# GpSimd's work in the token mixers in order of emission, stores issued by the engine that wrote them, and mixer transfers asked for some turns later

## Chip, cores and metric

The kernel runs on one core of one Trainium2 chip. The metric is the time of one execution on the device in microseconds; the number to beat is the median of three runs. Engines are named as in the profile: PE (matrix products), DVE (VectorE), ACT (ScalarE), POOL (GpSimd) and SP (SyncE, which here does nothing but issue transfers; SPq is its queue).

## What is computed

One layer of a hybrid encoder on a prompt of 512 frames and a sample of 64 frames, model width 2048, all in float32. The reference, cut to what matters here:

```python
def gdn_step(s, blk):            # 8 heads, 128 x 128 state
    q, k, v, g, beta = blk
    ...
    lower = jnp.where(strict, jnp.einsum('bhid,bhjd->bhij', kb, k) * decay, 0.0)
    rhs = jnp.concatenate([v * beta, kb * jnp.exp(big_g)[..., None]], axis=-1)
    sol = lax.linalg.triangular_solve(eye + lower, rhs, left_side=True, lower=True, unit_diagonal=True)
    ...

def token_mixers(h, ...):
    proj = h @ w_in
    ...
    o_a = from_heads(o_a, gla_norm) * jax.nn.silu(a_r)          # gated linear attention, 4 heads
    qkv, conv_new = causal_dwconv(concat([b_q, b_k, b_v]), st_conv, gdn_conv_w)
    q = l2norm(to_heads(c_q, GDN_HEADS)) * GDN_DK ** -0.5
    k = l2norm(to_heads(c_k, GDN_HEADS))
    ...
    o_b = from_heads(o_b, gdn_norm) * jax.nn.silu(b_g)          # gated DeltaNet, 8 heads
    return concat([o_a, o_b]) @ w_out, ...

def trunk(x, c, ...):
    mod = silu(c) @ w_ada + b_ada
    x = x + g1 * token_mixers(rmsnorm(x, norm1) * (1 + sc1) + sh1, ...)
    x = x + g2 * conv_ffn(rmsnorm(x, norm2) * (1 + sc2) + sh2, ...)
    return rmsnorm(x, final_norm), ...
```

## The kernel before

All activations are kept transposed, 128 features on the partitions by 2 x 288 frames (256 of the prompt and 32 of the sample in each half). A weight tile is loaded by SP, split by ACT into a high part and by DVE into a rest (lines 599 and 600), and each 128 x 128 tile takes six matmuls (`mm6`, lines 512 and 514): the "product matmuls" below.

The program has a head (modulation, normalization), then the mixer stage, then the output projection, and the FFN, in which nothing changes. In the mixer stage `in_tile` computes one projection tile of 128 columns after the other, 16 tiles of weights each, and calls `tick` after each of these 16. A tick gives one turn to the list of jobs (`job_step`) and now and then one step to the w_ada sums (`ada_block`: load 512 KB into one of two buffers `xr`, line 764, then four sums on DVE, line 772). A job is a generator, one for each head (`gdn` for the eight DeltaNet heads and for the sample, `gla` for the four attention heads). The list is walked from the oldest job; a job that yields WAIT lets the next one have the turn as well, a plain `yield` ends the turn. `rest(n)` yields WAIT n times: so many turns in which others run, while data gets ready.

For each DeltaNet head h the tiles come in the order q(h+1), k(h+1), v(h), gate(h), and q, k and v pass through `gdn_conv`: ACT and DVE copy the tile to `cb`, POOL sets its edges (lines 916 and 917) and saves its last columns (918, 919), then ACT (920), three sums on DVE (922), silu on ACT (924). A job of `gdn` then does this: a row of sums of log decays is loaded and made into decay matrices (ACT, POOL's selects 178 and 179); k and q are transposed (line 144), squared, and raised to -1/2 by POOL (`rsqrt`, lines 137 and 138); after a rest the block matrix `a` is made (216), and `inverse16` inverts its 32 diagonal 16 x 16 blocks: `a` is stored to DRAM (340), loaded as 32 lanes (345), worked on by POOL in 14 steps of two instructions (351, 352), copied (354), stored again (355) and loaded as columns `cm` (358), from which DVE builds two matrices (362). PE then joins the blocks to a whole inverse (238, 244, 253, 258), takes v (its transposes, 144), runs through four blocks of frames (276 to 305), and the outputs are squared, raised by POOL (138) to normalize them, transposed (144), multiplied by the gate and stored (`put_o`, 929), to be loaded again by `load_o` (1077) in the output projection. The sample's 64 columns of each tile go to DRAM by `put_s` (900), and are taken up by the jobs of the sample.

The order in which each engine issues its instructions is fixed when the program is built. A list scheduler takes instructions by priority (the order of emission, with weight splits and the jobs' DVE and ACT work moved ahead by 80) as soon as its own estimate says that they can run. Each engine then works strictly in that order, and so does each engine that issues transfers: an instruction that waits holds up everything behind it. All transfers stand in SP's queue.

Of the kernel before, what the change touches and what calls it, by code (L numbers as in the profile page):

```python
# [12 lines left out]
ALU = mybir.AluOpType  # L13
# [18 lines left out]
JOB_RATE, ADA_RATE = 1.0, 0.65  # L32


REST_D, REST_X, REST_T, REST_N, REST_G = 8, 16, 3, 2, 3
LATE = 3
N_EARLY = 4
N_EXTRA = 24
# [57 lines left out]
class Kern:  # L96
    def __init__(self, tc, ctx, i, o):
        self.tc, self.nc, self.ctx, self.i, self.o = tc, tc.nc, ctx, i, o
        self.n = 0
        self.cp = ctx.enter_context(tc.tile_pool(name="cp", bufs=1, side="left"))  # L100
        self.pg = ctx.enter_context(tc.tile_pool(name="pg", bufs=2, space=PSUM))
        self.c = {}
        self.jv, self.ja = _Sooner(tc, tc.nc.vector), _Sooner(tc, tc.nc.scalar)

    def load_consts(self, pool, names):
        nc = self.nc
# [28 lines left out]
    def rsqrt(self, out, src, n, parts=P):  # L135

        self.nc.vector.tensor_scalar_add(out[:parts, :n], src[:parts, :n], EPS)
        self.nc.gpsimd.tensor_tensor(out[:parts, :n], out[:parts, :n], self.mhalf[:parts, :n], op=ALU.pow)  # L138

    def transpose4(self, src4, n=4):  # L140

# [13 lines left out]
    def gdn(self, qF, kF, x, gain, hcols, gb_src, s0, s_out, o_put, last_level):  # L155
# [19 lines left out]
            A.activation(du[:, b], gb[:, b], AF.Relu, bias=gcol[:, b:b + 1], scale=-1.0)  # L175
        A.activation(dl, dl, AF.Exp, scale=-1.0)
        A.activation(du, du, AF.Exp, scale=-1.0)
        nc.gpsimd.affine_select(du, du, pattern=[[0, 4], [1, P]], compare_op=ALU.is_ge, fill=0.0, base=0, channel_multiplier=-1)
        nc.gpsimd.affine_select(dl, dl, pattern=[[0, 4], [-1, P]], compare_op=ALU.is_gt, fill=0.0, base=0, channel_multiplier=1)
        if pair:  # L180
            nc.gpsimd.memset(du[0:64, :, 64:P], 0.0)
        A.activation(gb, gb, AF.Exp)
        for b in range(4):
            A.activation(dl[:, b], dl[:, b], AF.Copy, scale=nbeta[:, b:b + 1])
# [136 lines left out]
        while "gate" not in x:  # L321
            yield WAIT
        V.tensor_tensor(kn, kn, x["gate"](), op=ALU.mult)
        o_put(kn)

    def rest(self, n):
# [4 lines left out]
    def inverse16(self, a):  # L331

        nc, c, G = self.nc, self.c, self.nc.gpsimd
        pitch = 4 * P
        d0 = self.dp.tile([8 * (16 * pitch + 16)], F32, tag="d0", bufs=2, name=self.name("d0"))
        d1 = self.dp.tile([2, 32, 256], F32, tag="d1", bufs=2, name=self.name("d1"))
        nc.sync.dma_start(d0[:P * pitch].rearrange("(p f) -> p f", p=P), a.rearrange("p b t -> p (b t)"))  # L340
        lane = self.m()[:32].rearrange("p (w f) -> p w f", w=2)
        xx, xt = [lane[:, n].rearrange("p (i j) -> p i j", i=16) for n in range(2)]
        blocks = d0.rearrange("(n f) -> n f", n=8)[:, :16 * pitch].rearrange("n (i b j) -> n i b j", i=16, b=4)
        for b in range(4):
            nc.sync.dma_start(xx[8 * b:8 * b + 8], blocks[:, :, b, :16])
        yield from self.rest(REST_D)
        G.memset(lane[:, 0, 0:256:17], 1.0)
        for i in range(1, 15):
            rest = slice(i + 1, 16)
            sh = [32, 15 - i, i]  # L350
            G.tensor_tensor(xt[:, rest, :i], xx[:, rest, i:i + 1].to_broadcast(sh), xx[:, i:i + 1, :i].to_broadcast(sh), op=ALU.mult)  # L351
            G.tensor_tensor(xx[:, rest, :i], xx[:, rest, :i], xt[:, rest, :i], op=ALU.add)  # L352
            yield WAIT
        G.tensor_copy(xt, xx.rearrange("p i j -> p j i"))
        nc.sync.dma_start(d1.rearrange("w q f -> q w f"), lane)
        cm = self.sp.tile([P, 2, 4, 16], F32, tag="cm", bufs=1, name=self.name("cm"))
        for w in range(2):
            nc.sync.dma_start(cm[:, w], d1[w].rearrange("(b n) (i j) -> (n i) b j", b=4, i=16))
        sh = [P, 4, 8, 16]
        t, u = self.m4(), self.m4()  # L360
        for w, x in enumerate((t, u)):
            nc.vector.tensor_tensor(x.rearrange("p b (n j) -> p b n j", n=8), cm[:, w].unsqueeze(2).to_broadcast(sh),
                                    c["bd16"].rearrange("p (n j) -> p n j", n=8).unsqueeze(1).to_broadcast(sh), op=ALU.mult)
        yield from self.rest(REST_X)
        return u, t

    def gla(self, nb, qF, kF, g, x, s0, s_out, o_put):
# [103 lines left out]
        for f in range(2):  # L471
            dst = (qd, kd3)[f]
            while f"gate{f}" not in x:
                yield WAIT
            V.tensor_tensor(dst, dst, x[f"gate{f}"](), op=ALU.mult)
            o_put(f, dst)


    def tick(self):
# [416 lines left out]
    def put_s(self, name, col, write):  # L896

        t = self.sp.tile([P, TS], F32, tag="ts", bufs=4, name=self.name("ts"))
        write(t)
        self.nc.sync.dma_start(self.sd[name][:, col * TS:(col + 1) * TS], t)  # L900

    def get_s(self, name, w=512):

# [4 lines left out]
    def gdn_conv(self, ps, t, dst, name, h):  # L908
# [4 lines left out]
        acc = self.ap.tile([P, 582], F32, tag="ca", bufs=1, name=self.name("ca"))  # L913
        A.activation(cb[:, 3:515].rearrange("p (h t) -> p h t", h=2), ps[:, :, :HP], AF.Copy)
        V.tensor_copy(cb[:, 518:582].rearrange("p (h t) -> p h t", h=2), ps[:, :, HP:HT])
        nc.gpsimd.tensor_copy(cb[:, 0:3], self.zero3)
        nc.gpsimd.tensor_copy(cb[:, 515:518], self.vmap["st_conv"].rearrange("p (i t) -> p t i", i=3)[:, t])
        nc.gpsimd.tensor_copy(self.cs[:, 0, :, t], cb[:, 512:515])
        nc.gpsimd.tensor_copy(self.cs[:, 1, :, t], cb[:, 579:582])
        A.activation(acc[:, :579], cb[:, 0:579], AF.Copy, scale=self.vec("gdn_conv_w", t))  # L920
        for j in range(1, 4):
            V.scalar_tensor_tensor(acc[:, :579], cb[:, j:j + 579], self.vec("gdn_conv_w", 24 * j + t), acc[:, :579],
# [701 lines left out]
        return g  # L1624


class _States:


# [55 lines left out]
```

## Time and profile before

| | before |
|---|---|
| three runs, us | 2977.28, 2977.57, 2982.16; median 2977.57 |
| the profiled execution, us | 2988.47, of which the span of the profile is 2986.8 |
| mean granted clock of PE | 0.978 |
| transfers | 395.55 MB, mean 132 GB/s |
| PE's busy tenths in 40 slices | 6998899999899999999999999999999999999998 |
| POOL's busy tenths | 0004342232210000000011011111101100000000 |

A row of the timeline gives start and length in us, engine, line, operation and tiles, then in brackets how long the engine was idle before it and what ended that. A row of the waits gives engine and line, what it waited for, the total in us, how often, and the longest. Line 1623 is the helper through which all DVE and ACT work of the jobs goes, so such work is told by its tiles.

### The profile page before, as it was taken

What the parts mean: (1) busy time and instruction counts of PE and PEld (TensorE: products, weight loads), DVE (VectorE), ACT (ScalarE), POOL (GpSimd) and SP (SyncE); (2) the same over time, 40 slices, a digit from 0 to 9 for tenths busy, and PEclk for the clock granted to TensorE, in tenths of its full rate; (3) what the DMA queues carried; (4) which work ended last, traced back from release to release, by engine and by line L of the source; (5) the groups of instructions that cost most, each with busy time, mean ns of one, the idle gap of its engine ahead of it and who ended that gap; (6) DMA issues with size and microseconds to landing.
All of it is one profiled execution on the core that took longest, in us unless ns stands there. A gap on an engine that the chain in (4) does not pass through costs nothing.

```text
span 2986.8 us, 52415 instructions
## 1 busy us (share of the span) xinstructions
PE 2871.2 (96%) x21096; PEld 2774.8 (93%) x21096; DVE 2048.5 (69%) x3198; ACT 1198.7 (40%) x2062; POOL 334.5 (11%) x609
## 2 busy tenths in 40 slices
PE   6998899999899999999999999999999999999998
PEld 3688889999799998999999999999999999999997
DVE  2355776667568867557888888888888865555555
ACT  4235454444435433245444444444444421222223
POOL 0004342232210000000011011111101100000000
PEclk7999999999899999999999999999999999999999
DMA  8964554445454446743333333333333473333221
GB/s 251 286 191 118 143 161 130 129 129 147 123 156 131 140 128 184 201 141 97 111 104 105 113 100 106 113 104 104 114 106 104 133 235 101 111 101 115 86 80 65
DMA packets 535446, 395.55 MB, mean 132 GB/s; under 512 B 59657, under 2 KB 465412, under 8 KB 535204
## 3 DMA queue, kind: packets, MB, share of 16 engines
q1 hardware_dynamic: 535204, 392.21, 44.7%
q8 instruction: 166, 2.72, 0.4%
q14 instruction: 76, 0.62, 0.1%
HBM read 356.47 MB, written 35.67 MB: 131 GB/s over the span
## 4 chain that ended last, share of the span: by engine, by line
PE 80%; DVE 6%; DMA 4%; POOL 4%; ACT 3%; issue 2%; SPq 0%; ACTq 0%; POOLq 0%; DVEq 0%
PE g L512 25%; PE g L514 13%; PE bank L1301 11%; PE bank L1300 11%; PE bank L1302 11%; DVE acc L772 2%; DMA xr<-in_w_ada_dram 1%; PE bank L144 1%; PE bank L672 1%; POOL m L352 1%; POOL m L351 1%; POOL s L138 1%; PE bank L405 1%; PE bank L778 1%; ACT m L1623 1%
## 5 line engine op out<-in xcount | busy, mean ns | idle before, releaser
L1301 PE MATMUL bank<-slot,wh 128*128 128x290 f32 x2464 | 736.2, 299 | 0.0
L1300 PE MATMUL bank<-slot,wh 128*128 128x290 f32 x2464 | 733.9, 298 | 0.0
L1302 PE MATMUL bank<-slot,wl 128*128 128x290 f32 x2464 | 728.0, 295 | 0.0
L512 PE MATMUL g<-slot,wh 128*128 128x288 f32 x3168 | 551.6, 295 | 0.2 <-DVE slot L1070 0.2
L512 PE MATMUL g<-hh,wh 128*128 128x288 f32 x2048 | 470.0, 308 | 2.4 <-ACT wh L599 2.4
L1302 PEld LDWEIGHTS bank<-slot,wl 128*128 128x128 f32 x2464 | 470.6, 191 | 0.0
L1301 PEld LDWEIGHTS bank<-slot,wh 128*128 128x128 f32 x2464 | 469.7, 191 | 0.1
L512 PEld LDWEIGHTS g<-slot,wh 128*128 128x128 f32 x3168 | 465.8, 188 | 0.7 <-DVE slot L1070 0.5
L1300 PEld LDWEIGHTS bank<-slot,wh 128*128 128x128 f32 x2464 | 464.1, 188 | 0.1
L514 PE MATMUL g<-hh,wl 128*128 128x288 f32 x2048 | 461.9, 304 | 1.2 <-DVE wl L600 1.2
L599 ACT ACTIVATE wh<-raw 128x1024 fp32r<-128x1024 f32 x215 | 227.2, 1058 | 586.6 <-PE g L512 571.4
L512 PE MATMUL g<-hl,wh 128*128 128x288 f32 x2048 | 460.6, 304 | 0.0
L1070 DVE SCALAR_TENSOR_TENSOR slot<-g,mod,slot 128x512 f32<-128x512 f32 (+1 forms) x448 | 201.9, 491 | 287.9 <-PE g L514 286.3
L772 DVE SCALAR_TENSOR_TENSOR acc<-xr,ct,acc 128x512 f32<-128x512 f32 x480 | 341.5, 754 | 29.0 <-DMA xr<-in_w_ada_dram 28.1
L512 PEld LDWEIGHTS g<-hh,wh 128*128 128x128 f32 x2048 | 337.7, 193 | 14.7 <-issue 10.2
L514 PEld LDWEIGHTS g<-hh,wl 128*128 128x128 f32 x2048 | 338.9, 193 | 8.3 <-issue 6.0
L514 PE MATMUL g<-slot,wl 128*128 128x288 f32 x1584 | 342.8, 295 | 0.0
L512 PEld LDWEIGHTS g<-hl,wh 128*128 128x128 f32 x2048 | 338.9, 193 | 4.1 <-issue 3.7
L600 DVE TENSOR_TENSOR wl<-raw,wh 128x1024 fp32r<-128x1024 f32 x215 | 262.0, 1219 | 64.9 <-ACT wh L599 63.3
L1247 ACT ACTIVATE wh<-raw 128x1024 fp32r<-128x1024 f32 x176 | 186.0, 1057 | 222.6 <-PE bank L1301 194.2
L514 PEld LDWEIGHTS g<-slot,wl 128*128 128x128 f32 x1584 | 255.3, 188 | 0.0
L1248 DVE TENSOR_TENSOR wl<-raw,wh 128x1024 fp32r<-128x1024 f32 x176 | 215.4, 1224 | 54.0 <-ACT wh L1247 54.0
(346 smaller groups left out, 3180.4 us busy)
## 6 DMA issues: line engine op xcount, KB each, us to landing
raw<-in_w_up_dram SPq DMA_DIRECT2D x176, 512.0 KB
xr<-in_w_ada_dram SPq DMA_DIRECT2D x128, 512.0 KB
raw<-in_w_in_dram SPq DMA_DIRECT2D x100, 512.0 KB
raw<-in_w_down_dram SPq DMA_DIRECT2D x88, 512.0 KB
hraw<-in_w_ada_dram SPq DMA_DIRECT2D x64, 512.0 KB
raw<-in_w_out_dram SPq DMA_DIRECT2D x32, 512.0 KB
slot<-actd SPq DMA_DIRECT2D x44, 288.0 KB
actd<-v SPq DMA_DIRECT2D x44, 256.0 KB
```

Source lines behind the costliest of these rows:

```text
L138: self.nc.gpsimd.tensor_tensor(out[:parts, :n], out[:parts, :n], self.mhalf[:parts, :n], op=ALU.pow)
L512: T.matmul(ps[:, h if bank is None else bank, :n], wh, x[:, h, :n], start=f, stop=False)
L514: T.matmul(ps[:, h if bank is None else bank, :n], wl, ah[:, h, :n], start=False, stop=stop)
L599: nc.scalar.activation(hi[:, :n_], raw[:, :n_], AF.Copy)
L600: nc.vector.tensor_tensor(lo[:, :n_], raw[:, :n_], hi[:, :n_].bitcast(F32), op=ALU.subtract)
L772: V.scalar_tensor_tensor(acc[s], w[:, k], col, acc[s], op0=ALU.mult, op1=ALU.add)
L1070: self.nc.vector.scalar_tensor_tensor(x1[:, :, z], ps[:, :, c], gain[:, q:q + 1], x1[:, :, z], op0=ALU.mult, op1=ALU.add)
L1247: self.nc.scalar.activation(hi, src, AF.Copy)
L1248: self.nc.vector.tensor_tensor(lo, src, hi.bitcast(F32), op=ALU.subtract)
L1300: T.matmul(ps, wh[:, j], hi, start=(c < 3 and j == 0), stop=False, skip_group_check=True)
L1301: T.matmul(ps, wh[:, j], lo, start=False, stop=False, skip_group_check=True)
L1302: T.matmul(ps, wl[:, j], hi, start=False, stop=(j == NPAIR - 1), skip_group_check=True)
```

## The change

POOL's work in the mixers goes through a helper, `_InTurn`, which ties each POOL instruction to the one emitted before it, so that the scheduler keeps them in the order of emission. The stores of `put_s` are issued by ACT, which wrote the tile (the log decays `ag`, which DVE writes, stay on SP), and the store of the inverted blocks by POOL. The rests around the transfers of `inverse16` are distributed anew: 2 turns before `a` is stored, 3 before it is loaded, 7 before POOL begins, 3 before the result is loaded, 5 before DVE uses it and 6 before PE does; before, these were 0, 0, 8, 0, 0 and 16. Five turns of rest stand before a head's output is stored. No computing instruction is added; 60 transfers change their engine.

```diff
-REST_D, REST_X, REST_T, REST_N, REST_G = 8, 16, 3, 2, 3
+REST_S, REST_L, REST_D, REST_X, REST_U, REST_T, REST_N, REST_O, REST_G = 2, 3, 7, 5, 6, 3, 2, 5, 3
...
         self.jv, self.ja = _Sooner(tc, tc.nc.vector), _Sooner(tc, tc.nc.scalar)
+        self.pool = _InTurn(tc, tc.nc.gpsimd)
...
-        self.nc.gpsimd.tensor_tensor(out[:parts, :n], out[:parts, :n], self.mhalf[:parts, :n], op=ALU.pow)
+        self.pool.tensor_tensor(out[:parts, :n], out[:parts, :n], self.mhalf[:parts, :n], op=ALU.pow)
...
         V.tensor_tensor(kn, kn, x["gate"](), op=ALU.mult)
+        yield from self.rest(REST_O)
         o_put(kn)
...
-        nc, c, G = self.nc, self.c, self.nc.gpsimd
+        nc, c, G = self.nc, self.c, self.pool
...
+        yield from self.rest(REST_S)
         nc.sync.dma_start(d0[:P * pitch].rearrange("(p f) -> p f", p=P), a.rearrange("p b t -> p (b t)"))
+        yield from self.rest(REST_L)
...
-        nc.sync.dma_start(d1.rearrange("w q f -> q w f"), lane)
+        G.dma_start(d1.rearrange("w q f -> q w f"), lane)
+        yield from self.rest(REST_L)
...
+        yield from self.rest(REST_X)
         t, u = self.m4(), self.m4()
...
-        yield from self.rest(REST_X)
+        yield from self.rest(REST_U)
         return u, t
...
-        self.nc.sync.dma_start(self.sd[name][:, col * TS:(col + 1) * TS], t)
+        (self.nc.sync if name == "ag" else self.nc.scalar).dma_start(self.sd[name][:, col * TS:(col + 1) * TS], t)
...
-        nc.gpsimd.tensor_copy(cb[:, 0:3], self.zero3)
+        self.pool.tensor_copy(cb[:, 0:3], self.zero3)
...
+class _InTurn:
+    def __init__(self, tc, engine):
+        self.tc, self.engine, self.last = tc, engine, None
+    def __getattr__(self, name):
+        f = getattr(self.engine, name)
+        def g(*a, **kw):
+            with self.tc.issue_after(self.last) if self.last is not None else nullcontext():
+                r = f(*a, **kw)
+            self.last = self.tc.nc.cur_bb.bb.instructions[-1]
+            return r
+        return g
```

The other calls of `nc.gpsimd` in `gdn` (selects and one memset) and in `gdn_conv` (the copies of lines 917 to 919) are replaced in the same way, and in `gla` the two output stores come together after the rest.

The first place where the order moves is POOL around the output norm of the second DeltaNet head. Before, its power (`s_546`) stands behind the end of the third head's inverse (`m_3489`):

```order
L352 TENSOR_TENSOR m_3489<-m_3489 32x3x12
L351 TENSOR_TENSOR m_3489<-m_3489 32x2x13
L352 TENSOR_TENSOR m_3489<-m_3489 32x2x13
L351 TENSOR_TENSOR m_3489<-m_3489 32x14
L352 TENSOR_TENSOR m_3489<-m_3489 32x14
L354 COPY m_3489<-m_3489 32x256
L138 TENSOR_TENSOR s_546_3687<-s_546_3687,mhalf 128x4
```

In the changed kernel the same power is called `s_545` and the third head's inverse `m_3741` (line 1648 is the helper, for all of POOL's mixer work):

```order
L1648 TENSOR_TENSOR rq_3297<-rq_3297,mhalf 128x4
L1648 COPY cb_3490<-zero_100 128x3
L1648 COPY cb_3490<-cols 128x3
L1648 COPY cs<-cb_3490 128x3 x2
L1648 TENSOR_TENSOR s_545_3681<-s_545_3681,mhalf 128x4
L1648 MEMSET m_3741 32x16
L1648 TENSOR_TENSOR m_3741<-m_3741 32x14 x2
```

The power has moved from behind the 28 steps and the copy of the inverse to ahead of its first instruction; it is so for all heads.

The second place is SP's queue after the lanes of the second head's inverse are asked for. Before, the store of the inverted blocks (`d_368`) and the load of the columns (`cm`) stand here, with loads of w_ada (`xr`) and w_in (`raw`) between them:

```order
L345 DMA m_2542<-d_367_2539 8x16x16 x4
L764 DMA xr_2743<-in_w_ada_dram 128x2x512
L764 DMA xr_2823<-in_w_ada_dram 128x2x512
L598 DMA raw_3389<-in_w_in_dram 128x8x128
L355 DMA d_368_2540<-m_2542 32x2x256
L764 DMA xr_2919<-in_w_ada_dram 128x2x512
L358 DMA cm_3107<-d_368_2540 128x4x16 x2
L764 DMA xr_2978<-in_w_ada_dram 128x2x512
```

Now, from just behind the load of the lanes on (lines are nine higher here and the load of `cm` is line 364):

```order
L773 DMA xr_2727<-in_w_ada_dram 128x2x512
L773 DMA xr_2811<-in_w_ada_dram 128x2x512
L773 DMA xr_2897<-in_w_ada_dram 128x2x512
L773 DMA xr_2971<-in_w_ada_dram 128x2x512
L773 DMA xr_3030<-in_w_ada_dram 128x2x512
L607 DMA raw_3377<-in_w_in_dram 128x8x128
L311 DMA out_dram<-st_2908 128x128
L773 DMA xr_3108<-in_w_ada_dram 128x2x512
L939 DMA od_71<-m_2092 256x1x256
L607 DMA raw_3507<-in_w_in_dram 128x8x128
L773 DMA xr_3287<-in_w_ada_dram 128x2x512
L364 DMA cm_3162<-d_366_2536 128x4x16 x2
```

The store has left the queue, and seven w_ada loads instead of three stand between the lanes and the columns.

The third place is POOL where the sixth head's k and q are normalized (`s_709`, `rq_4946`) and v of the fifth passes the convolution. Before (`cb_5147` is v's buffer):

```order
L919 COPY cs<-cb_4870 128x3
L916 COPY cb_5147<-zero_100 128x3
L917 COPY cb_5147<-cols 128x3
L138 TENSOR_TENSOR s_709_4921<-s_709_4921,mhalf 128x4
L138 TENSOR_TENSOR rq_4946<-rq_4946,mhalf 128x4
L918 COPY cs<-cb_5147 128x3
```

And now (`cb_5141` is v's buffer):

```order
L1648 AFFINE_SELECT m_4901<-m_4901 128x512
L1648 TENSOR_TENSOR s_709_4921<-s_709_4921,mhalf 128x4
L1648 TENSOR_TENSOR rq_4946<-rq_4946,mhalf 128x4
L1648 COPY cb_5141<-zero_100 128x3
L1648 COPY cb_5141<-cols 128x3
L1648 COPY cs<-cb_5141 128x3 x2
```

The two copies that set the edges of v's buffer have moved behind the powers of k and q. In PE's order the transposes of the sixth and seventh head's q and k stand 41 and 50 product matmuls later than before, and those of the fifth head's v 47 product matmuls behind the first of these, where it was 79.

More of the change, by code (lines that the diff above doesn't have):

```diff
@@ L177, in gdn @@
         A.activation(du, du, AF.Exp, scale=-1.0)
-        nc.gpsimd.affine_select(du, du, pattern=[[0, 4], [1, P]], compare_op=ALU.is_ge, fill=0.0, base=0, channel_multiplier=-1)
-        nc.gpsimd.affine_select(dl, dl, pattern=[[0, 4], [-1, P]], compare_op=ALU.is_gt, fill=0.0, base=0, channel_multiplier=1)
+        self.pool.affine_select(du, du, pattern=[[0, 4], [1, P]], compare_op=ALU.is_ge, fill=0.0, base=0, channel_multiplier=-1)
+        self.pool.affine_select(dl, dl, pattern=[[0, 4], [-1, P]], compare_op=ALU.is_gt, fill=0.0, base=0, channel_multiplier=1)
         if pair:
-            nc.gpsimd.memset(du[0:64, :, 64:P], 0.0)
+            self.pool.memset(du[0:64, :, 64:P], 0.0)
         A.activation(gb, gb, AF.Exp)
@@ L475, in gla @@
             V.tensor_tensor(dst, dst, x[f"gate{f}"](), op=ALU.mult)
-            o_put(f, dst)
+        yield from self.rest(REST_O)
+        for f in range(2):
+            o_put(f, (qd, kd3)[f])
     def tick(self):
@@ L915, in gdn_conv @@
         V.tensor_copy(cb[:, 518:582].rearrange("p (h t) -> p h t", h=2), ps[:, :, HP:HT])
[L916 to L919, printed above, removed]
+        self.pool.tensor_copy(cb[:, 0:3], self.zero3)
+        self.pool.tensor_copy(cb[:, 515:518], self.vmap["st_conv"].rearrange("p (i t) -> p t i", i=3)[:, t])
+        self.pool.tensor_copy(self.cs[:, 0, :, t], cb[:, 512:515])
+        self.pool.tensor_copy(self.cs[:, 1, :, t], cb[:, 579:582])
         A.activation(acc[:, :579], cb[:, 0:579], AF.Copy, scale=self.vec("gdn_conv_w", t))
```

## Prediction

> **What bounds the kernel now.** I read the shares of the page first, then busy time by stretch, then the matrix engine's (PE's) own gaps, then the rows of other engines around the largest gaps, and last the queue of SP.
>
> ```profile
> PE 2871.2 (96%) x21096; PEld 2774.8 (93%) x21096; DVE 2048.5 (69%) x3198; ACT 1198.7 (40%) x2062; POOL 334.5 (11%) x609
> 200.00:1300.00 1100.00, 1034.90 (x7585) 992.37 (x7584) 748.75 (x1307) 490.46 (x1113) 211.12 (x433) 0.97 0.52 146
> 1600.00:2000.00 400.00, 400.00 (x2976) 400.00 (x2975) 333.39 (x408) 179.84 (x214) 44.25 (x54) 1.00 0.37 106
> ```
>
> PE is the bound: 96% of the span. In the FFN (1600 to 2000 us; columns: length, then busy time and count of PE, weight loads, DVE, ACT, POOL, then granted clock, DMA share, GB/s) it has no gap, one matmul in 400/2976 = 0.134 us. The change touches the mixer stage alone, roughly 200 to 1300 us, where PE is idle for 1100 - 1034.9 = 65 us at a granted clock of 0.97. So the change can only work on those 65 us and on the clock there. These are the largest gaps (in brackets, idle time ahead and what ended it):
>
> ```profile
> 240.13 0.48 PE L144 MATMUL bank<-consts,m 128*128 128x128 f32 x1 [3.53 <-ACT m L1623]
> 280.57 0.48 PE L144 MATMUL bank<-consts,m 128*128 128x128 f32 x1 [5.46 <-ACT m L1623]
> 314.80 0.80 PE L276 MATMUL bank<-st,m 128*128 128x128 f32 x2 [6.13 <-DVE st L1623]
> 389.22 0.47 PE L144 MATMUL bank<-consts,m 128*128 128x128 f32 x1 [6.42 <-ACT m L1623]
> 454.88 0.44 PE L144 MATMUL bank<-consts,m 128*128 128x128 f32 x1 [2.57 <-ACT m L1623]
> 566.44 1.09 PE L144 MATMUL bank<-consts,qkv 128*128 128x128 f32 x8 [2.36 <-ACT qkv L924]
> 640.91 1.09 PE L144 MATMUL bank<-consts,qkv 128*128 128x128 f32 x8 [1.51 <-ACT qkv L924]
> 766.33 0.47 PE L144 MATMUL bank<-consts,m 128*128 128x128 f32 x1 [10.31 <-ACT m L1623]
> ```
>
> After a gap PE also runs slowly for some microseconds (the granted clock is the third number from the end):
>
> ```profile
> 314.80:319.40 4.60, 4.60 (x23) 4.55 (x24) 3.50 (x6) 1.67 (x8) 0.00 (x0) 0.61 0.36 92
> 389.20:393.80 4.60, 4.58 (x21) 4.57 (x22) 1.47 (x3) 1.53 (x4) 0.00 (x0) 0.53 1.05 263
> 454.90:458.50 3.60, 3.60 (x16) 3.58 (x17) 1.37 (x2) 3.02 (x7) 0.00 (x0) 0.53 0.27 38
> 766.30:772.30 6.00, 5.97 (x26) 5.96 (x27) 4.19 (x7) 1.54 (x4) 0.00 (x0) 0.50 0.50 153
> 566.40:574.40 8.00, 7.96 (x40) 7.96 (x41) 4.19 (x9) 4.11 (x21) 3.46 (x4) 0.57 0.68 195
> 642.00:650.00 8.00, 8.00 (x43) 7.98 (x42) 1.34 (x5) 3.89 (x19) 1.01 (x1) 0.57 0.25 67
> ```
>
> **Part 1: POOL in order of emission, and the inverse's store off SP's queue.** Two gaps show POOL's order directly. At 389 us:
>
> ```profile
> 381.62 0.27 DVE L137 TENSOR_SCALAR s<-s 128x4 f32<-128x4 f32 x1
> 387.15 0.59 POOL L354 COPY m<-m 32x256 f32<-32x256 f32 x1
> 387.72 1.01 POOL L138 TENSOR_TENSOR s<-s,mhalf 128x4 f32<-128x4 f32 x1
> ```
>
> The small power (line 138) that ends a head's output norm has its input at 381.9 and starts at 387.7, right behind the last instruction of the next head's 16x16 inverse. Four ACT copies and the transposes of PE wait for it. Now that power stands ahead of the whole inverse (first place shown in the order), so what is left is the chain itself, as where nothing blocked it:
>
> ```profile
> 835.31 0.33 PE L144 MATMUL bank<-consts,m 128*128 128x128 f32 x1 [0.78 <-ACT m L1623]
> ```
>
> So 389 gives 6.42 - 0.8 = 5.6 us. At 454 the pair stands alike in the chain of work:
>
> ```profile
> 452.81 0.59 POOL m L354
> 453.40 0.99 POOL s L138
> ```
>
> 2.57 - 0.8 = 1.8 us. Two gaps come by way of SP:
>
> ```profile
> 743.73 0.37 SPq L598 DMA_DIRECT2D raw<-in_w_in_dram  x1
> 758.26 0.33 SPq L355 DMA_DIRECT2D d<-m  x1
> 758.68 0.38 SPq L764 DMA_DIRECT2D xr<-in_w_ada_dram  x1
> 762.82 1.41 DVE L772 SCALAR_TENSOR_TENSOR acc<-xr,ct,acc 128x512 f32<-128x512 f32 x2 [9.01 <-DMA xr<-in_w_ada_dram]
> 313.07 1.41 DVE L772 SCALAR_TENSOR_TENSOR acc<-xr,ct,acc 128x512 f32<-128x512 f32 x2 [6.46 <-DMA xr<-in_w_ada_dram]
> ```
>
> SP issues nothing for 14 us, until the inverse is finished and its store (L355) can go; the load of w_ada stands behind that store, DVE stands still 9.0 us for the load, and behind DVE's wait stands the norm that PE waits for. The same at 313 us (6.5 us). The store is now issued by POOL, behind its own copy, and SP has seven w_ada loads ahead of the load that needs it (second place). I take both gaps as gone but for the chain: 10.31 - 0.8 = 9.5 and 6.1 us. Idle time won: 5.6 + 1.8 + 9.5 + 6.1 = **23.0 us**. The slow clock behind these four, length times what is missing to 1: 4.6 x 0.39 + 4.6 x 0.47 + 3.6 x 0.47 + 6.0 x 0.50 = 1.8 + 2.2 + 1.7 + 3.0 = **8.7 us**.
>
> **Part 2: stores of the sample columns from ACT.** 51 stores move from SP to ACT, and the nine of the inverse to POOL.
>
> ```profile
> SPq L355 <- POOL m L354: 74.5, 8, 14.0
> SPq L900 <- ACT ts L925: 35.0, 16, 4.0
> SPq L358 <- DMA d<-m: 10.7, 8, 3.0
> ```
>
> (SP's waits: total, times, longest.) SP loses the first two waits. ACT pays at most 51 x 0.33 (the issue at 758.26) = 17 us, in a stage in which it is busy 490 of 1100 us; I cost it at nothing, hidden beside PE, and at 17 us if every store stood ahead of something PE waits for. A store from POOL is not in the trace. Nearest rows: landing of the same store from SP, 10.7/8 = 1.3 us to 3.0 us. I take 3 us. Its cover: the inverse's result is ready here (two products on DVE) long before PE first uses it,
>
> ```profile
> 393.03 1.29 DVE L362 TENSOR_TENSOR m<-cm,consts 128x512 f32<-128x512 f32 x2 [0.28 <-DMA cm<-d]
> 421.96 1.00 PE L238 MATMUL bank<-m,m 128*128 128x64 f32 x8
> ```
>
> 27.6 us, so nothing; without cover, 9 x 3.0 = 27 us. The Trainium skill (SBUF — State Buffer, "SBUF: two separate sides") says of a DMA issued by GpSimd that its descriptors cannot be written while VectorE runs a two-port operation, and that such a DMA belongs on ACT or SP. It gives 3.1 us for one held so; nine would be 28 us, an estimate from that page, on the same cover. No row here shows such a store.
>
> **Part 3: the rests.** From the block matrix to the first use of the inverse the rests come to 2+3+7+3+5+6 = 26 turns, before 8+16 = 24, and five are added ahead of the output store. A turn is six product matmuls, 0.8 us. Two turns before the use delay only when PE does that work, not how much it does. The five at the end lie here:
>
> ```profile
> 1173.72 2.52 SPq L934 DMA_DIRECT2D od<-m  x4
> 1261.28 5.29 SPq L1077 DMA_DIRECT2D raw<-od  x2
> ```
>
> The last store of head outputs goes 87 us before the next loads of them, against 4 us of rest: nothing. But PE's order shifts: the transposes of a new head's q and k (gaps at 566 and 641) stand 41 and 50 product matmuls later, 5.5 and 6.7 us, more than they waited. They could give 2.36 + 1.51 plus the clock of two windows, 2 x 8.0 x 0.43 = 6.9, in all 10.8 us. I take half, **5.4 us**, since their input (the convolution of k) now stands behind the exponentials on ACT, whose load may be late in SP's queue. The gaps of heads 0 and 1 at 240 and 281 us (9.0 us) hang on DVE, ACT and POOL together, and the power of q still stands behind the first inverse; I take a third, **3 us**.
>
> **What it adds.** POOL's strict order puts the first two copies of v's convolution (L916, L917) behind the powers of the next head's k and q (third place). Before:
>
> ```profile
> 565.88 1.02 POOL L916 COPY cb<-zero 128x3 f32<-128x3 f32 x1 [5.49 <-DVE ca L922]
> 573.54 1.01 POOL L138 TENSOR_TENSOR rq<-rq,mhalf 128x4 f32<-128x4 f32 x1 [2.52 <-DVE rq L137]
> 584.19 0.77 ACT L920 ACTIVATE ca<-cb,cols 128x579 f32<-128x579 f32 x1
> 589.62 0.63 ACT L924 ACTIVATE qkv<-ca 128x512 f32<-128x512 f32 x1 [4.66 <-DVE ca L922]
> 590.30 0.66 PE L144 MATMUL bank<-consts,qkv 128*128 128x128 f32 x4
> ```
>
> The power of q ends 574.55 - 566.44 = 8.1 us after the transposes of q and k begin. Two copies, 0.4 to 2.0 us; then from L920 to the end of L924 6.1 us: v is ready 14.6 to 16.2 us after them. PE comes to v's transposes after 47 product matmuls (79 before), 6.3 us, and the head's own matmuls. Those took 23.9 - 79 x 0.134 - 3.4 of slow clock = 9.9 us before. So PE arrives at 16.2 us, with 0 to 1.6 us to spare. With DVE's other work in between I expect about 1 us of waiting for seven heads, and 2 us of slow clock behind two of them: 7 + 4 = **11 us** lost; bounds 0 and 40 (4 us and half the heads' clock).
>
> **Sum.** 23.0 + 8.7 + 5.4 + 3 - 11 = 29 us of the profiled span of 2986.8. That execution took 2988.47, 0.37% over the median of 2977.57; scaled by that, 29 stays 29: **2948 us**.
>
> **Rivals.**
> - *All of it goes well*: parts 1 and 3 in full and no wait for v: 23.0 + 8.7 + 10.8 + 9.0 = 51.5 us, 2926. For it: SP's queue is nearly free of waits. Against: a tight chain for v in each head.
> - *SP's wait only moves*: the load of the inverse's result (L358) still stands in SP's queue and waits for POOL's chain and the slower store, with weights and w_ada behind it. If that brings back the gaps at 314 and 766, 6.1 + 9.5 + 1.8 + 3.0 = 20.4 us return: gain 9, 2969. Against: it is asked for three turns after the store.
> - *Only issue time is saved*: 60 issues of 0.33 us on engines beside PE, nothing on the path, and new gaps for old: 2977. The Trainium skill (DMA: Bandwidth & Descriptors, "Issuing engines are not separate DMA queues") says that spreading DMAs over engines saves just the time to issue them. The 74.5 us above speak against it: here the queue's order is what waits.
> - *v late, slower*: POOL holds v's copies longer than PE leaves room. At 4 us for seven heads and 3.4 us of slow clock behind each, 52 us instead of 11: 12 us slower, 2989. It decides from 2.4 us for each head on (7 x 5.8 us is the whole gain).
>
> **How the numbers follow.** About 0.2% (6 us) can be told from no change. Forecast (gain of 15 to 42 us) 0.52; all goes well 0.16; SP's wait moves 0.16; only issue time 0.06; v late 0.10. Faster 0.84, same 0.06, slower 0.10. The range reaches from 2926, the first rival, to 2974, past the second; it leaves out the last two and little below.
>
> **What would show it.** Right: no gap over 2 us ahead of a head's last transposes (L144 behind the power); no DVE wait for w_ada behind the inverse; SP's waits for POOL a fraction of 74.5 us; PE idle in the stage near 40 us instead of 65, clock 0.98 or more. Wrong: gaps ahead of the transposes of v released by L924, POOL's copies L916 starting late behind L138, or SP standing long at L358.

## Result and the profile after

The change made the kernel **slower by 0.6%**: 2997.61 us (median of four runs, 2996.68 to 2998.48) beside 2979.86 us of the kernel before on the same chip, ratio 1.0062 with a 95% interval of [1.0046, 1.0078]. The prediction was 2948 us with a range to 2974 and 0.84 for faster; it was wrong in sign. The profiled execution took 2998.38 us with a span of 2996.7, which is 9.9 us more than the profiled execution of before. The medians lie 17.8 us apart, since the profiled execution of before lay 8.6 us above this median and that of the changed kernel 0.8 us above its own.

In the changed kernel lines stand some higher: the transposes (144) are 146, the row load (170) is 172, the inverse's store, lanes and columns `cm` (340, 345, 358) are 344, 350 and 364, DVE's products of `cm` (362) are 369, w_ada's load and sums (764, 772) are 773 and 781, and the convolution (914, 915, 920, 922, 924) is 924, 925, 930, 932 and 934. Line 1633 is the jobs' DVE and ACT work, and 1648 all of POOL's mixer work.

First the busy time by stretch of the changed kernel (columns as in the prediction: length, busy time and count of PE, weight loads, DVE, ACT, POOL, granted clock, DMA share, GB/s), for the stage and for 8 us behind two gaps:

```profile
200.00:1300.00 1100.00, 1025.78 (x7488) 983.63 (x7487) 744.44 (x1296) 480.32 (x1105) 221.54 (x442) 0.96 0.50 144
578.50:586.50 8.00, 8.00 (x36) 8.00 (x37) 4.11 (x8) 3.23 (x13) 0.92 (x1) 0.50 0.65 184
742.80:750.80 8.00, 7.99 (x51) 7.99 (x51) 2.28 (x5) 3.99 (x16) 1.03 (x1) 0.72 0.47 131
```

PE is idle 74.2 us in the stage (1100 - 1025.78) instead of 65.1, and the clock is a hundredth lower instead of higher. What PE and the others wait for (changed kernel; total, times, longest):

```profile
PE bank L146 <- ACT qkv L934: 35.3, 7, 8.5
PE bank L146 <- ACT m L1633: 11.3, 12, 3.8
SPq L364 <- DMA d<-m: 68.2, 9, 10.2
ACT m L1633 <- DMA m<-gd: 33.7, 7, 9.6
DVE m L369 <- DMA cm<-d: 43.6, 10, 7.9
DVE acc L781 <- DMA xr<-in_w_ada_dram: 16.2, 21, 1.9
```

The same waits in the kernel before:

```profile
PE bank L144 <- ACT m L1623: 33.4, 13, 10.3
PE bank L144 <- ACT qkv L924: 5.4, 3, 2.4
ACT m L1623 <- DMA m<-gd: 10.3, 5, 3.2
DVE m L362 <- DMA cm<-d: 15.3, 5, 6.1
DVE acc L772 <- DMA xr<-in_w_ada_dram: 28.1, 17, 9.0
```

The last transposes' wait for the normalized output fell by 22.1 us, as meant. This is what became of the gaps at 389, 454 and 766 us (PE of the changed kernel):

```profile
380.78 0.33 PE L146 MATMUL bank<-consts,m 128*128 128x128 f32 x1 [1.19 <-ACT m L1633]
454.39 0.33 PE L146 MATMUL bank<-consts,m 128*128 128x128 f32 x1 [0.79 <-ACT m L1633]
776.54 0.33 PE L146 MATMUL bank<-consts,m 128*128 128x128 f32 x1 [0.69 <-ACT m L1633]
```

The wait of the next head's k and q transposes for the convolution of k (L934) rose by 29.9 us. How that came, in the head around 510 to 580 us, from the timelines of PE, POOL, SP, DVE and ACT of the changed kernel (start, length, engine; idle time ahead in brackets):

```profile
578.48 1.97 PE L146 MATMUL bank<-consts,qkv 128*128 128x128 f32 x8 [7.19 <-ACT qkv L934]
...
532.23 1.01 POOL L1648 TENSOR_TENSOR s<-s,mhalf 128x4 f32<-128x4 f32 x1 [19.90 <-DVE s L139]
533.25 5.93 POOL L1648 TENSOR_TENSOR m<-m 32x14 f32<-32x14 f32 x16
547.39 1.45 POOL L1648 COPY cs<-cb 128x3 f32<-128x3 f32 x2 [7.20 <-ACT cb L924]
548.79 8.03 POOL L1648 TENSOR_TENSOR m<-m 32x54 f32<-32x54 f32 x12
557.79 0.62 POOL L1648 DMA_DIRECT2D d<-m  x1 [0.29 <-POOL m L1648]
...
520.66 1.40 SPq L350 DMA_DIRECT2D m<-d  x4
548.86 0.37 SPq L607 DMA_DIRECT2D raw<-in_w_in_dram  x1
559.79 0.37 SPq L364 DMA_DIRECT2D cm<-d  x1
561.87 0.53 SPq L172 DMA_DIRECT2D m<-gd  x1
...
561.72 1.30 DVE L369 TENSOR_TENSOR m<-cm,consts 128x512 f32<-128x512 f32 x2 [5.56 <-DMA cm<-d]
567.74 0.22 DVE L925 COPY cb<-g 128x64 f32<-128x64 f32 x1
...
568.00 0.99 ACT L1633 ACTIVATE m<-m,ncum 128x128 f32<-128x128 f32 x3 [7.90 <-DMA m<-gd]
573.35 0.76 ACT L930 ACTIVATE ca<-cb,cols 128x579 f32<-128x579 f32 x1
```

POOL stands idle 19.9 us for the power of the older head (`s<-s,mhalf`), whose input is ready only at 532, although the lanes of the next head's inverse were asked for at 520.7. The inverse starts behind that power, is cut in two by the edge copies of the next q tile (7.2 us for its copy by ACT), and ends at 557.5. The load of `cm` goes at 559.8, 39 us after the lanes. SP stood there from 549 on, and the next head's row (L172) goes behind it. DVE waits for `cm` in front of its copy for k's convolution (L925), and ACT for the row in front of the convolution's next step (L930). In the kernel before the inverse ran ahead of that power (timelines of POOL and SP):

```profile
515.89 0.12 POOL L347 MEMSET m<- 32x16 f32 x1 [2.31 <-DMA m<-d]
525.40 0.62 POOL L354 COPY m<-m 32x256 f32<-32x256 f32 x1
526.62 1.01 POOL L138 TENSOR_TENSOR s<-s,mhalf 128x4 f32<-128x4 f32 x1 [0.60 <-DVE s L137]
...
512.57 1.64 SPq L345 DMA_DIRECT2D m<-d  x4
527.79 0.36 SPq L358 DMA_DIRECT2D cm<-d  x1
```

There `cm` was loaded 15 us after the lanes. In the four heads whose lanes are asked for between 430 and 690 us it was 15 to 17 us there, and 37 to 43 us in the changed kernel.

### The profile page after: what moved, and what is told of

It reads as the page before. It is cut to its first block, busy times and chain, and to the rows that moved or that the text cites. A ratio compares the mean times of both kernels' runs of the same rounds, so it can differ in the third digit from the quotient of the medians.

```text
span 2996.7 us, 52397 instructions
## 1 busy us (share of the span) xinstructions
PE 2870.9 (96%) x21096; PEld 2776.8 (93%) x21096; DVE 2050.4 (68%) x3198; ACT 1193.1 (40%) x2060; POOL 345.6 (12%) x618
## 4 chain that ended last, share of the span: by engine, by line
PE 76%; issue 6%; DMA 5%; DVE 4%; POOL 4%; ACT 3%; SPq 1%; ACTq 0%; POOLq 0%; DVEq 0%
PE g L521 24%; PE g L523 12%; PE bank L1311 11%; PE bank L1310 11%; PE bank L1312 11%; POOL m L1648 2%; DVE acc L781 2%; DMA xr<-in_w_ada_dram 2%; PE bank L146 1%; PE bank L681 1%; ACT m L1633 1%; POOL s L1648 1%; PE bank L412 1%; PE bank L787 1%; DVE wl L609 1%
## 5 line engine op out<-in xcount | busy, mean ns | idle before, releaser
L781 DVE SCALAR_TENSOR_TENSOR acc<-xr,ct,acc 128x512 f32<-128x512 f32 x480 | 339.4, 751 | 16.3 <-DMA xr<-in_w_ada_dram 16.2
L523 PEld LDWEIGHTS g<-hh,wl 128*128 128x128 f32 x2048 | 336.4, 192 | 10.3 <-issue 5.9
```

The lines of the kernel that those rows point to most:

```text
L523: T.matmul(ps[:, h if bank is None else bank, :n], wl, ah[:, h, :n], start=False, stop=stop)
L781: V.scalar_tensor_tensor(acc[s], w[:, k], col, acc[s], op0=ALU.mult, op1=ALU.add)
```

## Experiments

Each ratio is to the kernel before on the same chip, with its 95% interval. The waits are totals in us from the profiled execution: PE for k's convolution (L934), PE for the last transposes' input (L1633), ACT for the row, DVE for `cm`, DVE for w_ada; "-" is none. Line numbers differ by a few between the kernels; the columns follow the work. The row's 25.1 in e11 counts 6.7 us that a split of weights on ACT waited for it. The medians come from several chips, so the ratios are what compares.

| kernel | median, us | ratio | k conv | last tr. | row | cm | w_ada |
|---|---|---|---|---|---|---|---|
| before | 2979.86 | 1 | 5.4 | 33.4 | 10.3 | 15.3 | 28.1 |
| after | 2997.61 | 1.0062 [1.0046, 1.0078] | 35.3 | 11.3 | 33.7 | 43.6 | 16.2 |
| e1 order alone | 2979.45 | 0.9986 [0.9973, 0.9999] | 20.0 | 12.3 | 7.1 | 17.8 | 14.9 |
| e2 stores alone | 2991.30 | 1.0022 [1.0007, 1.0036] | 7.6 | 41.8 | 10.0 | 18.1 | 39.0 |
| e3 rests alone | 2983.19 | 0.9999 [0.9987, 1.0011] | - | 41.9 | 8.4 | 12.2 | 29.0 |
| e4 cm by POOL | 3006.23 | 1.0064 [1.0042, 1.0085] | 30.5 | 12.9 | 7.5 | 67.0 | 20.4 |
| e5 cm read later | 2999.13 | 1.0056 [1.0041, 1.0071] | 39.1 | 12.3 | - | - | 41.4 |
| e6 conv copies free | 3022.92 | 1.0137 [1.0120, 1.0154] | 25.5 | 16.9 | 25.8 | 54.0 | 40.7 |
| e7 no order | 2980.27 | 0.9994 [0.9983, 1.0006] | 7.0 | 28.4 | 7.3 | 7.9 | 28.2 |
| e8 e4 and e5 | 2982.17 | 1.0001 [0.9992, 1.0011] | 27.7 | 12.0 | 0.3 | - | 15.8 |
| e9 inverse free | 2984.33 | 1.0018 [1.0004, 1.0032] | 14.1 | 32.9 | 8.7 | 11.1 | 29.2 |
| e10 e9, cm later | 2993.25 | 1.0052 [1.0033, 1.0071] | 4.6 | 31.9 | 9.6 | - | 14.5 |
| e11 power inside | 2966.11 | 0.9951 [0.9932, 0.9969] | 12.3 | 5.6 | 25.1 | 17.9 | 26.5 |
| e12 e8, edges by DVE | 3003.65 | 1.0081 [1.0053, 1.0110] | 45.3 | 11.2 | 2.2 | - | 17.3 |
| e13 order, stores | 3000.96 | 1.0064 [1.0049, 1.0079] | 27.5 | 17.3 | 26.1 | 23.7 | 25.8 |
| e14 order, rests | 3003.91 | 1.0069 [1.0053, 1.0085] | 30.6 | 11.3 | 26.2 | 39.3 | 33.0 |
| e15 e11, stores on SP | 2958.80 | 0.9924 [0.9909, 0.9939] | 4.9 | 8.3 | 9.2 | 10.9 | 27.3 |
| e16 e11, cm later | 2967.30 | 0.9946 [0.9930, 0.9963] | 7.0 | 7.9 | 0.4 | - | 18.4 |

### One part of the change at a time

e1 is the kernel before with `self.pool = _InTurn(tc, nc.gpsimd)` used for all of POOL's mixer work. e2 has the two edits of stores, e3 all edits of rests:

```diff
+        (self.nc.sync if name == "ag" else self.nc.scalar).dma_start(self.sd[name][...], t)   # e2
+        nc.gpsimd.dma_start(d1.rearrange("w q f -> q w f"), lane)                             # e2
+REST_S, REST_L, REST_D, REST_X, REST_U, REST_T, REST_N, REST_O, REST_G = 2, 3, 7, 5, 6, 3, 2, 5, 3   # e3
```

> Before, with POOL's mixer work put in order of emission and nothing else (all stores on SP, old rests). Theory A (the strict order stretches the inverse, so that the load of cm is late; it stands in SP's queue just ahead of the next head's row load at L172, and ACT, with the relus of that row queued inside k's convolution, makes PE's next transposes wait): the gaps ahead of the last transposes go, PE's waits for the bank of L146 released by L934 rise from 5.4 us to 25 or more, time 2985 to 3000 us. Rival B (the order is good and the rests do the harm): those waits stay under 10 us, time 2950 to 2965. Rival C (the stores do the harm): as B, 2950 to 2965.

> Before, with only the stores moved: put_s to ACT, the inverse's store to POOL. Theory A: SP's 74.5 us behind POOL become a wait of the same length at the load of cm, PE's waits for L934 stay near 5 to 12 us, time 2972 to 2984. Rival B: same as A, it says nothing of the stores. Rival C (issuing on ACT and POOL costs more than it frees): ACT's 51 issues and POOL's 9 show as PE waits for ACT, time 2990 or more.

> Before, with only the rests of after. Theory A: the kq transposes come as late as in after, but with POOL's old order the inverse is not stretched, so the row load is in time: PE's waits for L934 under 12 us, time 2968 to 2982. Rival B (the rests alone push the relus and exponentials into k's convolution on ACT): PE's waits for L934 at 25 us or more, time 2990 or more. Rival C: 2968 to 2982.

The fourth takes `cm` out of SP's queue, in the changed kernel:

```diff
-            nc.sync.dma_start(cm[:, w], ...)
+            G.dma_start(cm[:, w], ...)
```

> After, with the two loads of cm issued by POOL, right behind its own store, so that SP never stands at them; POOL's order, rests and the other stores as in after. Theory A: ACT's waits for the row (33.7 us) fall to about 10, PE's waits for L934 from 35.3 us to about 10, time 2998 less some 25 to 35 with the clock behind them: 2963 to 2975. Rival B: the waits for L934 stay at 25 us or more, time 2990 to 3000. Rival C (issuing by POOL costs): time 2998 or more.

None of the parts alone makes the loss. The order alone (e1, between theory A's numbers and the rivals') gives what it was meant to, 33.4 to 12.3 us, and takes back most of it at k's convolution. With the stores alone SP's 74.5 us at L355 are found again one step on, added to the 10.7 us that it had waited there before, and the sum of 85.2 us is no shorter (waits of e2):

```profile
SPq L358 <- DMA d<-m: 92.1, 9, 14.4
```

The time of e2 is rival C's, but its reason does not show: what rose are DVE's waits for w_ada, which stands behind that load (28.1 to 39.0), and PE's for the last transposes (33.4 to 41.8). These are two of PE's gaps in e2:

```profile
324.60 0.48 PE L144 MATMUL bank<-consts,m 128*128 128x128 f32 x1 [8.83 <-ACT m L1623]
769.40 0.47 PE L144 MATMUL bank<-consts,m 128*128 128x128 f32 x1 [6.71 <-ACT m L1623]
```

The first stands behind a wait of DVE for w_ada (7.6 us, up to 321.7) and has taken the place of the 6.1 us at 314. The second, 10.3 us at 766 before, does not: the power (767.9) stands on POOL behind the inverse and its store (767.2), and DVE has its w_ada only at 775. With the order alone both are gone: no wait for the last transposes' input is longer than 3.0 us in e1, though the store is still in SP's queue and SP waits 46.0 us for POOL there. The rests alone (e3) gave the waits that theory A had, in a time 1.2 us above its range.

e4 was a miss for theory A; rival B's waits came, in rival C's time: ACT's wait for the row fell to 7.5 us as theory A said, but PE's did not, and the time stayed. The timelines of DVE and ACT of e4 show why:

```profile
572.65 1.45 DVE L369 TENSOR_TENSOR m<-cm,consts 128x512 f32<-128x512 f32 x2 [9.21 <-DMA cm<-d]
...
569.60 0.99 ACT L1633 ACTIVATE m<-m,ncum 128x128 f32<-128x128 f32 x3 [2.34 <-DMA m<-gd]
577.64 0.78 ACT L930 ACTIVATE ca<-cb,cols 128x579 f32<-128x579 f32 x1 [2.59 <-DVE cb L925]
```

ACT has its row now, and then waits for DVE's copy (L925), which stands behind the two products of a `cm` that is as late as before. So theory A had one of two waits.

### Reading cm later, freeing the copies, no order

e5 is the changed kernel with `REST_X, REST_U = 11, 0` instead of 5, 6. e6 takes the convolution's four copies out of the order (`nc.gpsimd.tensor_copy`), e7 the whole order (`self.pool = tc.nc.gpsimd`).

> After, with two rests changed (REST_X 5 to 11, REST_U 6 to 0): by the programs' order DVE's two products of cm (L369) then stand behind the sums of the next k's convolution (L932) instead of ahead of them, and SP's next row load (L172) stands ahead of the load of cm (L364). POOL's order is the same as in after. Theory A, mended after the fourth run (the late cm holds two engines in front of k's convolution, DVE at L369 and, through SP's queue, ACT at the row; freeing one is not enough): PE's waits for L934 fall from 35.3 us to under 12, time 2963 to 2980. Rival D (POOL's own order makes k late, since its edge copies of the convolution stand behind the inverse's steps): those waits stay at 20 us or more, time 2990 to 3000.

> After, with the four edge and state copies of the convolution left to the scheduler's place on POOL; powers, selects and the inverse stay in order of emission. Theory A: the inverse no longer waits for the next q tile (4.8 us in one head of the fourth run), and the order puts L369 ahead of q's convolution on DVE; cm still comes after the head's power, so some of the wait goes to q: PE's waits for L934 10 to 25 us, time 2980 to 2995. Rival D: the waits for L934 fall under 10 us, time 2965 to 2980.

> After without the order of emission on POOL: the moved stores and the rests stay. Theory A: the inverse is as short as before, PE's waits for L934 under 10 us, but the waits for the last transposes' input come back (33 us before): time 2975 to 2992, about what the stores alone and the rests alone gave together. Rival D: the same. A rival on which the stores and the rests are the harm (E): 2993 or more.

e7 undoes the loss: without the order the stores and the rests cost nothing together, so rival E is out. The order is needed for the loss, but e1 shows that it is not enough. e5 was the second miss: the waits for the row and for `cm` are gone, and PE waits longer. The numbers are rival D's, but ACT stands 12.2 us for the edges on POOL and 51.6 us for DVE's copy. Timelines of SP, DVE and ACT of e5:

```profile
563.73 1.74 SPq L364 DMA_DIRECT2D cm<-d  x2
565.59 0.43 SPq L773 DMA_DIRECT2D xr<-in_w_ada_dram  x1
...
569.66 2.74 DVE L781 SCALAR_TENSOR_TENSOR acc<-xr,ct,acc 128x512 f32<-128x512 f32 x4 [8.98 <-DMA xr<-in_w_ada_dram]
...
573.77 0.78 ACT L930 ACTIVATE ca<-cb,cols 128x579 f32<-128x579 f32 x1 [10.87 <-DVE cb L925]
```

SP still stands at `cm`, w_ada stands behind it, and DVE waits for w_ada in front of the same copy: a third way. e6 missed too, and so did rival D in it: with the copies free DVE's products come ahead of q's convolution in four of the heads, and DVE waits 54.0 us for `cm` and 40.7 for w_ada. PE waits 15.8 us for ACT's splits of weights as well, 1.9 in the changed kernel.

### All three ways freed, and the inverse free

e8 is e4 and e5 together. e9 leaves only the inverse's own instructions on POOL out of the order (`G = self.nc.gpsimd`), e10 is e9 with the rests 11, 0.

> After, with the two edits that failed alone put together: both loads of cm issued by POOL, and the rests 11 and 0, so that DVE's products stand behind k's sums. Theory A, mended again after the fifth run: a late cm reaches k's convolution by three waits (DVE at L369; SP at L364 with the next row behind it, for ACT; SP at L364 with w_ada behind it, for DVE at L781), and any one that is left is enough. With all three gone PE's waits for L934 fall under 12 us, DVE's for w_ada to 15 or so, time 2965 to 2982. Rival F: cm itself is what comes too late, so that the wait only moves on to the blocks' joins (L240, L246) and the head's own chain: waits for L934 low but PE's waits there 20 us or more, time 2990 to 3000. Rival D (POOL's order on the convolution's edges): waits for L934 stay at 20 or more, 2990 to 3000.

> After, with the inverse's memset and its steps on POOL left to the scheduler's place, its store still issued by POOL; powers, selects and the convolution's copies stay in order of emission. By the programs' order the inverse then begins ahead of the head's power, not behind it. Theory A: cm is early again, PE's waits for L934 fall under 12 us; the power stands some steps ahead of the inverse's end, so the last transposes keep most of what they gained (11 to 20 us of waits for L1633): time 2962 to 2978. Rival F: same as A here. Rival G (one queue, two clients: what the inverse gains the power loses): waits for L1633 go back to 28 us or more, 2976 to 2986. Rival D: waits for L934 at 20 or more, 2990 or more.

> The kernel before this one with the rests 11 and 0 as well. Theory A: with cm early, where it is read costs nothing either way: within 4 us of the run with the inverse free, unless its cm is still late in some heads, when this is 5 to 10 us faster. Rival F: the later read makes the joins late, 5 to 10 us slower.

e8 wins back the whole loss (2982 us, ratio 1.0001), which two edits that did nothing alone could only do if each left another way open. It did not beat the kernel before, and the waits for k stayed at 27.7, not under 12. PE's idle time in the stage fell by 9.7 us, to 64.5, and 7.6 of them are the wait for k. Waits of e8:

```profile
ACT ca L930 <- POOL cb L1648: 37.4, 9, 8.8
```

The edge copies on POOL are a fourth way, as rival D had it (its waits came, its time did not). The edit adds to it: k's edges stand on POOL behind the load of `cm`, for which POOL now waits 22.1 us in 7 places; in the changed kernel ACT stood 20.5 us for the edges. e9 showed rival G: the inverse is early, PE's wait for k falls to 14.1, and the power is late again (32.9). e10 missed by 9 us: there the joins of the blocks wait for DVE (9.5 us, 0.4 in e9), as rival F said, and two waits of PE for ACT's tile `sq` (line 291) add 9.4 us, which rival F did not say; the wait for k falls by 9.5.

### The power inside the inverse; the edges on DVE

e11 keeps the order of the changed kernel and moves places in it, so that POOL works on the inverse while it would stand idle for the power:

```diff
-REST_S, REST_L, REST_D, REST_X, ... = 2, 3, 7, 5, ...
+REST_S, REST_L, REST_D, REST_X, ... = 2, 3, 1, 11, ...
...
             A.activation(junk, ops[:, b], AF.Square, scale=float(P) ** -0.5, accum_out=ss[:, b:b + 1])
+        yield from self.rest(12)
         self.rsqrt(rr, ss, 4)
```

e12 is e8 with the convolution's four copies issued by DVE (`V.tensor_copy`).

> After, with the inverse begun sooner and the head's power asked for later (REST_D 7 to 1, REST_X 5 to 11, twelve rests ahead of the power of the output norm), so that in POOL's order of emission the memset and seven pairs of the inverse's steps stand ahead of the power of the head before, and the other seven behind it. In after POOL stood idle 19.9 us for that power (512.3 to 532.2 us) while the inverse's lanes had been asked for at 520.7. Theory A: the inverse runs in that idle time, cm comes 8 to 15 us sooner, and all three waits of the run before last go without any load being moved: PE's waits for L934 under 12 us, those for L1633 stay near 11, time 2958 to 2975. Rival D: the edge copies still stand behind the steps, waits for L934 15 us or more, 2980 to 2992. Rival H: later powers make the head's last transposes and its gate late, with waits for L1633 of 25 us or more, 2980 or more.

> The kernel with all three waits freed (cm loaded by POOL, rests 11 and 0), with the convolution's four small copies moved from POOL to DVE. There ACT still stood 37.4 us for the edges on POOL (9 times). Rival D, as what is left after theory A's waits: PE's waits for L934 fall from 27.7 us to under 10, time 2962 to 2975. Theory A alone: they stay at 20 or more, 2978 to 2985. Rival K (96 more instructions on DVE, in an order of their own, cost what they free): waits for DVE's splits rise, 2982 or more.

e11 is faster than both kernels, at 2966.11 us, within theory A's 2958 to 2975. Its wait for k is 12.3 us, where theory A had under 12. e12 was a miss: the time is rival K's, but not its sign, since PE waits for DVE's splits no longer than in e8 (1.7 and 1.8 us). The wait for edges on POOL is gone, and 81.1 us of waits of ACT for POOL's selects of the next head take its place. Timelines of POOL and ACT of e12:

```profile
552.97 1.51 POOL L1648 DMA_DIRECT2D cm<-d  x2 [4.66 <-DMA d<-m]
554.49 1.24 POOL L1648 TENSOR_SCALAR_AFFINE_SELECT m<-m 128x512 f32<-128x512 f32 x2
...
555.76 1.28 ACT L1633 ACTIVATE m<-m,nbeta 128x128 f32<-128x128 f32 x4 [12.31 <-POOL m L1648]
```

The selects stand behind the inverse and its transfers: a fifth way from the same late inverse to k's convolution.

### Pairs, and what the fast version needs

e13 is order and stores with the old rests, e14 order and rests with every store on SP, e15 is e11 with every store on SP, e16 is e11 with the rests 17 and 0 in the place of 11 and 6.

> Before with POOL's order of emission and the moved stores, with the old rests. Theory A with the pair order and rests: twelve pairs of steps stand ahead of q's edges as in the run of the order alone, so PE's waits for L934 stay near the 20 us of that run, time 2973 to 2985. Rival S (order and stores are the pair): 35 us or more of those waits, 2990 or more.

> After with every store back on SP: order of emission and rests. Theory A with the pair order and rests: eight pairs ahead of q's edges, the late cm as in after, PE's waits for L934 30 us or more, time 2990 to 3002. Rival S: waits of 20 or less, 2972 to 2985.

> The fastest version so far (2966 us) with every store back on SP. Theory A: what made it fast is POOL's order alone; SP then waits at the inverse's store instead of at cm's load, at almost the same place in its queue: 2960 to 2972. Rival: a store that waits on SP holds w_ada and weights longer: 2975 to 2985.

> The fastest version with the rests 17 and 0 in the place of 11 and 6: DVE's two products of cm (for which it still waited 17.9 us in 6 places, 10.4 at most) stand behind the sums of k's convolution. Theory A: those waits go, 3 to 8 us faster than 2966, 2958 to 2964. Rival F: the blocks' joins wait for DVE instead, as in the run with the inverse free and these rests (5 us slower or more): 2970 to 2980.

The order loses 0.6 to 0.7% with either of the other parts, and both together are no worse, so there was no one pair to find: e13 came out in rival S's time and e14 in theory A's waits. What tells the order alone from these three is ACT's wait for the row, 7.1 us there and 26.1, 26.2 and 33.7 in them. That the rests do this by leaving eight pairs of steps ahead of q's edges instead of twelve fits e14; e13 has twelve and loses too, so it is not the only reason. Nor is it how late `cm` is: in five heads from 440 us on it is asked for 31 to 44 us after the lanes in e1, and 33 to 37 us in e13. Why the stores are enough stays open.

e15 is the fastest, 2958.80 us, 0.8% under the kernel before and 1.2 us below theory A's range. The moved stores gave nothing in it; whether they cost something can't be said, since the intervals of e11 and e15 touch. The stage in the busy time by stretch of e15:

```profile
200.00:1300.00 1100.00, 1055.44 (x7777) 1012.85 (x7776) 765.85 (x1334) 501.52 (x1135) 219.02 (x436) 0.98 0.53 149
```

Its waits (line 1634 is the jobs' work):

```profile
PE bank L146 <- ACT m L1634: 8.3, 5, 3.1
PE bank L146 <- ACT qkv L935: 4.9, 4, 2.0
```

And the head of 510 us in its timelines of POOL (line 1649) and SP (365 is the load of `cm`):

```profile
510.40 0.12 POOL L1649 MEMSET m<- 32x16 f32 x1 [14.26 <-DMA m<-d]
510.47 5.53 POOL L1649 TENSOR_TENSOR m<-m 32x14 f32<-32x14 f32 x14
518.16 1.01 POOL L1649 TENSOR_TENSOR s<-s,mhalf 128x4 f32<-128x4 f32 x1 [2.17 <-DVE s L139]
519.15 6.25 POOL L1649 TENSOR_TENSOR m<-m 32x56 f32<-32x56 f32 x14
532.49 0.63 POOL L1649 COPY m<-m 32x256 f32<-32x256 f32 x1
...
535.85 0.92 SPq L365 DMA_DIRECT2D cm<-d  x2
539.61 0.42 SPq L172 DMA_DIRECT2D m<-gd  x1
```

Half of the inverse runs before the power, for whose input POOL now stands only 2.2 us. The lanes were asked for at 507.4, so `cm` goes 28.4 us and the next row 32.2 us behind them, in the changed kernel 39.1 and 41.2. In the four heads named above `cm` is still 28 to 36 us behind its lanes, about twice as long as in the kernel before, and 7 to 11 us sooner than in the changed kernel; PE waits only 4.9 us for k. PE is idle 44.6 us in the stage instead of 74.2. e16 missed, in a time between theory A's and rival F's: the waits for `cm` and the row went, and the joins waited 9.4 us for DVE instead.

## Why the prediction was wrong

- **The step that failed is in Part 1**: "Now that power stands ahead of the whole inverse (first place shown in the order), so what is left is the chain itself". That prices one of POOL's two customers. The order that lets the power go first also holds the inverse until the power's input is there, and the place in the order shows this as plainly as the gain. The gain came as worked out: the gaps at 389, 454 and 766 became 1.19, 0.79 and 0.69 us and that at 314 went, 22.7 of the 23.0 us. The price was put at nothing and was 29.9 us of new waits for k, 14.6 of them with the order alone (e1). e7 shows that the loss needs the order (without it the loss is gone), and e11 and e15, which keep the order and let half of the inverse go ahead of the power, that it is the inverse's wait and not the order as such. They move the power and the rests by hand, so what each of these edits gives alone is not shown.
- **Part 1's second cause** did not bear its 15.6 us. The gaps at 314 and 766 were laid to the inverse's store in SP's queue. The order alone closes both with the store still there (e1), and the moved store alone leaves 8.8 and 6.7 us (e2). That these two terms came out is luck.
- **Part 2's cover** was measured to the wrong reader. "27.6 us, so nothing" is the time from DVE's products to PE's use. But DVE and SP read `cm` at a fixed place in their own orders, with k's convolution, w_ada and the next row behind them; there the readers stood up to 7.9 us (DVE) and 9.6 us (ACT). The stores alone cost 0.2%, 6.6 us by the ratio, of the 17 us I gave as the bound of ACT's issues (e2). Where these lie is not shown, since the two profiled executions differ by 0.6 us; what the profile of e2 shows is that SP's wait moved and stayed. A store from POOL landed after 2.0 us, less than the 3 I took. The Trainium skill's rule that spreading DMAs over engines saves just their issue time (DMA: Bandwidth & Descriptors, "Issuing engines are not separate DMA queues") agrees with that run better than my argument against it: SP's waits at the store and the load behind it, 74.5 and 10.7 us, became 92.1, and no time was won.
- **Part 3** named the mechanism and drew the wrong sign from it. It said of k's convolution that it "now stands behind the exponentials on ACT, whose load may be late in SP's queue", and took half of a 10.8 us gain for it. That gap was the one that grew. The gain is real where the inverse is early: with the rests alone the wait for k is gone (e3).
- **What it adds**: v never made PE wait; all seven gaps behind L934 are those of k's and q's transposes. The 11 us were taken at the wrong tile. The third of 9.0 us for heads 0 and 1 was too little: the gap at 281 went, that at 240 stayed (3.8 us).
- **The clock**: 8.7 us were to come back behind closed gaps. New gaps took their place, with 0.50 and 0.72 behind two of them, so nothing came back: the stage's clock went from 0.97 to 0.96.
- **The rivals**: *SP's wait only moves* had the place, SP standing at the load of `cm` (68.2 us), and among the signs of a wrong prediction SP "standing long at L358" was the one that came. It had the price wrong: I let it bring back the old gaps at 314 and 766, and did not ask what else stood behind it. The slower case I wrote was another one.

None of the parts alone moved the time by more than 0.2%: 0.9986, 1.0022 and 0.9999. Shown is that a late `cm` reaches k's convolution by several waits at once: removing one of them left the loss as it was (e4, e5), removing two won it back (e8), and removing a third in e8 opened another and lost it again (e12). Not settled is why the order alone loses nothing and loses 0.6% with either of the others.

## What to carry to other kernels

A fixed order on an engine with two customers has two prices: before putting one first, read when its input is ready, and count what the engine could have done for the other until then. Cover is measured to the reader's place in its own engine's order, not to the last use of the data. And when a late result feeds several in-order queues, freeing one of them shows nothing; move the result, or free all of them in one run.

## What the runs showed of the hardware

- A store of 64 KB issued by POOL landed 2.0 us after its issue in the median of nine (changed kernel), and POOL waited 0.7 to 4.9 us for it where it also issued the load behind it (e4, e8, e12). In one of e4, 4.65 us up to 570.36, DVE stood idle all the while (its 9.21 us above), so VectorE's two-port operations, the cause that the Trainium skill names for a late DMA of GpSimd (SBUF — State Buffer, "SBUF: two separate sides"), were not the cause there; what was stays open.
- The inverse's steps on POOL took almost twice as long in one half as in the other in the changed kernel: 16 instructions in 5.93 us, then 12 in 8.03 (0.37 and 0.67 us each), and 28 in 9.5 us before (0.34 each, 515.9 to 525.4). DVE was busy 1.44 us of the first stretch, 6.87 us of the second and 2.60 us of the one before the change. It is so in the other heads: in both kernels together, the steps took 0.33 to 0.46 us each where DVE was busy at most 0.41 of the stretch, and 0.60 to 0.71 where it was busy 0.83 or more. So an inverse that is put beside a busy DVE comes later still. POOL's spans are rough, and what of DVE's work slows the steps is not shown.
